# Spreading two q loads of a rotary-embedding score kernel unevenly over the sixteen DMA engines

## The chip, the cores and the metric

The kernel runs on one core of a Trainium2 chip. The core has TensorE (PE) with its weight loads (PEld), VectorE (DVE), ScalarE (ACT), GpSimd (POOL) and SyncE (SP), and sixteen DMA engines that move data between the chip's memory and the core's on-chip memory. SP, ACT and POOL issue DMAs; the sixteen engines carry them out. The metric is the time of one execution on the device in microseconds: the median of five runs.

## The reference

q and k are 16 batches x 512 positions x 16 heads x 64 floats. Both get a rotary embedding (cos and sin per position, 32 each), and then, for every batch and every position s, the 16 heads at s are multiplied with the head vectors of k. The `einsum` pairs equal heads only, so each batch and head gives a 512 x 512 matrix of scores over positions.

```python
q1, q2 = q[..., :half_dim], q[..., half_dim:]
q_rot = np.concatenate([q1 * cos_q - q2 * sin_q,
                        q1 * sin_q + q2 * cos_q], axis=-1)
...                                            # k_rot in the same way
scores = np.einsum('bshd,bthd->bsht', q_rot, k_rot)
```

The inputs are 2 x 32 MiB, the output 256 MiB, all float32: 67 MB are read and 268 MB written.

## The kernel before, in words

**Tiling.** A batch of q or k lies in on-chip memory as 128 partitions (rows) x 4 slots x 1024 floats: position 4p + c is row p, slot c. A row of a whole load is therefore 16 KB that lie together in memory, and a slot of a row is 4 KB. There are two buffers for q and two for k (`inb`, L219), used in turn by batch: batch 1 and batch 3 share a buffer, and so on.

**Steps.** There are 64 steps, one for each slot of each batch. In a step `scores` (L392) makes eight pairs of matmuls (L409), ACT copies each pair from PSUM to a stage buffer `st` (L418), and after the eighth copy SP issues one store of 4 MB (L426). There are three stage buffers; a copy into one waits until the store that used it before has landed. In the first four steps (batch 0) the store is cut into four of 1 MB (L422), and two of the stage buffers are in use. Beside this, DVE applies the embedding to slots for later steps (`rope`, L335: two products and a sum of 1.2 us each), and PE transposes them (L360), with copies from PSUM by DVE or ACT (L378).

**Loads.** Batch 0 comes in four smaller loads (`load_units`, L247). Batches 1 and up come whole, by `load` (L264), 2 MB each, on SP's queue among the stores: k and q of batch 1 at the start (L441, L442), the others when a buffer comes free (L475, L482, L508, L510). SP works in the order of the program: a DMA behind one that waits is issued later. What has been issued on SP's queue is carried out on each DMA engine in that order.

**Rows and engines.** A whole load or store of 128 rows puts 8 rows on each of the sixteen engines. A load with another number of rows is spread over fewer engines when the count doesn't divide by 16. The kernel uses this for four q loads (`RELIEVED`, L260: batches 5, 8, 11 and 14). There GpSimd issues the load of 120 rows, each as two halves of 8 KB (`halves`, L289), in its own queue (q0 in the profile), beside SP's queue (q1). A tiny load of five rows ahead of it (`move_cursor`, L282) makes GpSimd's spreading begin at engine 5, so that the fifteen engines 5 to 15 and 0 to 3 get eight rows each and engine 4 (`SLOW`, L262) none. The last 8 rows come in two ways: for batches 5 and 11 (even count) SP loads them (L302), one row each on eight engines; for 8 and 14 (odd count) GpSimd loads them ahead of the 120, after a tiny load of eight rows, on engines 8 to 15 (L296 to L298).

**Waits.** Every operation is put on a list with keys that it reads and writes, and `Plan.resolve` (L38) works out from them who waits for whom. The keys of a loaded buffer are made per slot: `in` for the rows of the main load, `in rest` for the remaining ones; a reader of a slot waits for both (`src_keys`, L304).

Of the kernel before, what the change touches and what calls it, by code (L numbers as in the profile page):

```python
# [7 lines left out]
PE, ACT, DVE, POOL, SP = "PE", "ACT", "DVE", "POOL", "SP"  # L8
# [170 lines left out]
def kernel(  # L179
# [8 lines left out]
    nc = tc.nc  # L188
# [4 lines left out]
    B, S, H, D = q.shape  # L193
    HD = D // 2
    P = 128
    C = S // P
# [9 lines left out]
    dram = {  # L206
        "q": q.rearrange("b (p c) h d -> b p c h d", c=C),
        "k": k.rearrange("b (p c) h d -> b p c h d", c=C),
    }
# [19 lines left out]
    def one(f):  # L229
        def emit():  # L230
            a = f()
            return a, a

        return emit

    def dma(engine, e, dst, src, sem, reads=(), writes=(), also=()):
        plan.add(engine, one(lambda: e.dma_start(dst, src)), reads, writes, sem=sem, also=also)  # L237
# [22 lines left out]
    RELIEVED = {("q", 5): 0, ("q", 8): 1, ("q", 11): 2, ("q", 14): 3}  # L260
# [3 lines left out]
    def load(which, b):  # L264
        if b >= B:
            return
        t = inb[which][b % 2]
        sem = f"in_{which}{b % 2}"
        rows = [("in", which, b % 2, c) for c in range(C)]
        rest = [("in rest", which, b % 2, c) for c in range(C)]  # L270
        if (which, b) not in RELIEVED:
            dma(SP, nc.sync, t.rearrange("p c (h d) -> p c h d", h=H), dram[which][b], sem, writes=rows + rest)
            return

        n, E, F = 120, C * H * D, C * H * D // 2
        x = RELIEVED[which, b]
        d = dram[which][b]  # L280

        def move_cursor(k):  # L282
            y = tiny[0]
            tiny[0] += 1
            src = bass.AP(q.tensor, 512 * y, [(512, k), (64, 2), (1, 2)])
            dst = scratch[:k, 4 * y : 4 * y + 4].rearrange("p (a b) -> p a b", a=2)
            dma(POOL, nc.gpsimd, dst, src, "cursor", writes=[("scratch", y)])

        def halves(lo, hi, keys, sem):  # L289
            src = bass.AP(d.tensor, d.offset + lo * E + F, [(E, hi - lo), (-F, 2), (1, F)])  # L290
            v = t[lo:hi]
            dst = bass.AP(v.tensor, v.offset + F, [(v.ap[0][0], hi - lo), (-F, 2), (1, F)])
            dma(POOL, nc.gpsimd, dst, src, sem, writes=keys)

        plan.add(POOL, None, (), rows)
        if x % 2:  # L296
            move_cursor(8)
            halves(n, P, rest, f"rest{x}")  # L298
        move_cursor(SLOW + 1)
        halves(0, n, rows, f"part{x}")  # L300
        if not x % 2:
            dma(SP, nc.sync, t[n:].rearrange("p c (h d) -> p c h d", h=H), d[n:], sem, writes=rest)  # L302

    def src_keys(which, n):  # L304
        if n < C:
            return [("unit", which, n)]
        return [(name, which, n // C % 2, n % C) for name in ("in", "in rest")]

    def src_also(which, n):
        return unit_keys(which, n) if n < C else ()  # L310
# [1 line left out]
    def rope(which, n):  # L312
# [9 lines left out]
        else:  # L322
# [7 lines left out]
            adds = [(x4, swapped)]  # L330
        xs, xc = x.rearrange(sv, **k2), x.rearrange(sv, **k1)
        keys, more = src_keys(which, n), src_also(which, n)

        def tt(o, a, b, op, reads, writes):
# [14 lines left out]
    def transposed(which, n, g, engine):  # L349
        m = banks[0] % 2  # L350
        banks[0] += 1
        bank = ps_t[m]
        if n < C:
            srcs = [units[which, n][:, x, P * g : P * (g + 1)] for x in range(4)]
        else:
            t = inb[which][n // C % 2]
            srcs = [t[:, n % C, P * (4 * g + x) : P * (4 * g + x + 1)] for x in range(4)]

        def emit():
            done = [nc.tensor.transpose(bank[:, x, :], srcs[x], ident) for x in range(4)]  # L360
            return done[0], done[-1]

        plan.add(PE, emit, src_keys(which, n) + ["ident"], [("bank", m)], also=src_also(which, n))
        src = bank
        if which == "q":
            dst = qTb[n % 2][:, 4 * g : 4 * g + 4, :]
            keys = [("qT", n % 2, 4 * g + x) for x in range(4)]
        else:
            b = n // C
            if n < C:  # L370
                dst = kTb[b % 2][:, 2 * n + g].rearrange("p (t c) -> p t c", c=C)
                src = bank.rearrange("p c t -> p t c")
                keys = [("kT", b % 2, 2 * n + g, c) for c in range(C)]
            else:
                dst = kTb[b % 2][:, 4 * g : 4 * g + 4, P * (n % C) : P * (n % C + 1)]
                keys = [("kT", b % 2, 4 * g + x, n % C) for x in range(4)]
        copy = nc.scalar.copy if engine == ACT else nc.vector.tensor_copy
        plan.add(engine, one(lambda: copy(out=dst, in_=src)), [("bank", m)], keys)  # L378
# [59 lines left out]
    for head, heads in ((0, G), (G, H - G)):  # L438
        load_units("k", head, heads)
        load_units("q", head, heads)  # L440
    load("k", 1)  # L441
    load("q", 1)  # L442
    plan.add(POOL, one(lambda: nc.gpsimd.memset(ident, 0.0)), (), ["ident"])
    plan.add(
# [15 lines left out]
    for i in range(C):  # L460
        plan.step = i
        if i < C - 1:
            dve = rope("k", i + 1) + rope("q", i + 1) + rope("k", C + i)
            nxt = [("k", i + 1), ("q", i + 1)]
        else:
            dve = rope("q", C) + rope("k", C + i) + rope("q", C + 1) + rope("k", 2 * C)
            nxt = [("q", C), ("k", C + i)]
        for p in range(HP):
            scores(i, p)
            if p in (0, 1) and i > 0:  # L470
                run(dve[:1])
                dve = dve[1:]
                transposed("k", C + i - 1, p, DVE)
            if p == 3 and i < 2:
                load("kq"[i], 2)  # L475
            if p in (2, 6):
                m = len(dve) - (4 if p == 2 else 2) - (2 if i == C - 1 else 0)
                run(dve[:m])
                dve = dve[m:]
                tr_act(*nxt.pop(0))  # L480
        run(dve)
# [65 lines left out]
```

## Time and profile before

| what | us |
|---|---|
| median of 5 runs | 799.25 (798.51 to 799.48) |
| profiled execution: its own time | 799.38 |
| profiled execution: span from first to last instruction | 797.6 |
| PE busy / ACT busy / DVE busy | 685.0 / 562.7 / 545.2 |
| SP's waits for ACT's copies ahead of stores | 715.8 |
| from issue to landing, median: 4 MB store / 2 MB load of q on SP | 25.6 / 29.3 |
| from issue to landing, median: 120-row load by GpSimd | 32.1 |

How to read it: a busy time is the sum over an engine's instructions. The profile's DMA row gives for 40 equal slices of the span the mean busy share of the sixteen DMA engines in tenths, 9 standing for 90% or more, and the row below it the GB/s that they moved. The queue table gives packets, megabytes and the share of sixteen engines' span that the packets took. The chain of waits goes back from the last instruction to what released it, step by step. The table by stage gives for each stretch its length, each engine's busy time and number of instructions, the granted TensorE clock, the DMA share and GB/s. All times count from the first instruction of the span. The trace also holds a record of each DMA packet: its queue, start, duration and bytes, though not the engine that carried it, and the time of each engine's report of a landed DMA.

### The profile page before, as it was taken

The page shows a single profiled execution, that of the slowest core. Times are in us where ns is not written, and L with a number is a line of the kernel's source. Part 1 is how long each engine was busy: PE and PEld are TensorE (multiplying, and loading weights), DVE is VectorE, ACT ScalarE, POOL GpSimd, SP SyncE. Part 2 cuts the span into 40 slices and gives each one's busy share as a digit, 9 for nine tenths or more (in the row PEclk, how much of TensorE's full clock was granted, in tenths as well). Part 3 has the DMA queues.
Part 4 walks back from the last instruction along what each step waited for, and adds up shares of the span by engine and source line. Part 5 has one row for each costly group of instructions (what it writes and reads, how often), then busy time and mean ns, then how long its engine had stood idle before and what let it go on. Part 6 is the DMA issues. An engine that isn't in the chain of part 4 may idle for free.

```text
span 797.6 us, 8197 instructions
## 1 busy us (share of the span) xinstructions
PE 685.0 (86%) x3072; PEld 296.2 (37%) x3072; DVE 545.2 (68%) x516; ACT 562.7 (71%) x647; POOL 8.4 (1%) x18
## 2 busy tenths in 40 slices
PE   3989999888988979899797997979879799789960
PEld 2444444333433434344343443434334344334420
DVE  6999988566776768568585775858758488575400
ACT  2978887775867768488585785868757687677860
POOL 0000000000000000100000000000000100000000
PEclk9999999997998999899898898989989899998995
DMA  9999999999999999999999999999999999999995
GB/s 343 420 423 438 428 415 422 430 428 432 427 419 429 435 431 431 431 428 410 433 427 439 426 438 428 418 433 432 432 429 432 431 427 414 427 439 411 436 425 247
DMA packets 18513, 335.87 MB, mean 421 GB/s; under 512 B 2128, under 2 KB 3408, under 8 KB 4432
## 3 DMA queue, kind: packets, MB, share of 16 engines
q1 hardware_dynamic: 16832, 327.42, 96.4%
q0 software_dynamic: 1376, 8.13, 2.4%
q10 hardware_dynamic: 288, 0.13, 0.1%
q8 instruction: 6, 0.10, 0.0%
q14 instruction: 11, 0.09, 0.0%
HBM read 67.24 MB, written 268.44 MB: 421 GB/s over the span
## 4 chain that ended last, share of the span: by engine, by line
DMA 47%; PE 37%; DVE 6%; ACT 6%; issue 1%; ACTq 0%; DVEq 0%; SPq 0%
DMA out_dram<-st 47%; PE ps L409 28%; PE bank L360 9%; ACT st L418 6%; DVE part L335 2%; DVE st L335 2%; DVE k_sb L335 1%; DVE q_sb L335 1%; DMA sin_t<-in_sin_dram 0%; DVE kT L378 0%; DVE qT L378 0%; ACTq L237 0%; ACT ss_t L455 0%; ACT ss_t L454 0%; ACTq L110 0%
## 5 line engine op out<-in xcount | busy, mean ns | idle before, releaser
L418 ACT COPY st<-ps 128x1024 f32<-128x1024 f32 x512 | 495.9, 1018 | 196.7 <-DMA out_dram<-st 101.2
L409 PE MATMUL ps<-kT,qT 64*128 64x512 f32 x2048 | 542.9, 646 | 71.7 <-ACT st L418 71.5
L409 PEld LDWEIGHTS ps<-kT,qT 64*128 64x128 f32 x2048 | 182.2, 195 | 261.4 <-issue 131.6
L378 DVE COPY qT<-bank 128x512 f32<-128x512 f32 x118 | 81.5, 691 | 197.5 <-PE bank L360 197.5
L360 PEld LDWEIGHTS bank<-ident,q_sb 128*128 128x128 f32 x480 | 55.3, 151 | 101.7 <-issue 98.2
L360 PE MATMUL bank<-ident,q_sb 128*128 128x128 f32 x480 | 86.4, 307 | 1.0 <-DVE q_sb L335 1.0
L360 PEld LDWEIGHTS bank<-ident,k_sb 128*128 128x128 f32 x480 | 50.5, 141 | 93.4 <-DVE k_sb L335 45.8
L360 PE MATMUL bank<-ident,k_sb 128*128 128x128 f32 x480 | 78.7, 287 | 1.2 <-DVE qT L378 0.8
L378 ACT COPY kT<-bank 128x512 f32<-128x512 f32 x122 | 72.4, 597 | 6.7 <-PE bank L360 6.7
L335 DVE TENSOR_TENSOR part<-q_sb,ss_t 128x1024 f32<-128x1024 f32 x60 | 73.5, 1225 | 3.2
L335 DVE TENSOR_TENSOR k_sb<-k_sb,cos_t 128x1024 f32<-128x1024 f32 x60 | 73.5, 1225 | 2.0
L335 DVE TENSOR_TENSOR q_sb<-q_sb,cos_t 128x1024 f32<-128x1024 f32 x60 | 73.5, 1225 | 2.1
L335 DVE TENSOR_TENSOR k_sb<-k_sb,part 128x1024 f32<-128x1024 f32 x60 | 73.5, 1225 | 2.1
L335 DVE TENSOR_TENSOR part<-k_sb,ss_t 128x1024 f32<-128x1024 f32 x60 | 72.9, 1216 | 0.3
L335 DVE TENSOR_TENSOR q_sb<-q_sb,part 128x1024 f32<-128x1024 f32 x60 | 72.9, 1215 | 0.0
L360 PE MATMUL bank<-ident,st 128*128 128x128 f32 x64 | 10.7, 317 | 13.3 <-DVE st L335 13.3
L360 PEld LDWEIGHTS bank<-ident,st 128*128 128x128 f32 x64 | 8.3, 161 | 18.7 <-DVE st L335 17.7
L335 DVE TENSOR_TENSOR part<-st,ss_t 128x1024 f32<-128x1024 f32 x8 | 9.8, 1223 | 6.4 <-ACT ss_t L455 6.0
L335 DVE TENSOR_TENSOR st<-st,part 128x512 f32<-128x512 f32 x16 | 11.0, 690 | 0.5
L237 POOL DMA_DIRECT2D scratch<-in_q_dram x6 | 3.6, 600 | 616.0 <-PE bank L360 616.0
L335 DVE TENSOR_TENSOR st<-st,cos_t 128x1024 f32<-128x1024 f32 x8 | 9.8, 1225 | 0.3
L378 ACT COPY qT<-bank 128x512 f32<-128x512 f32 x10 | 5.7, 616 | 3.5 <-PE bank L360 3.5
(11 smaller groups left out, 11.0 us busy)
## 6 DMA issues: line engine op xcount, KB each, us to landing
out_dram<-st SPq DMA_DIRECT2D x60, 4096.0 KB, 25.6
k_sb<-in_k_dram SPq DMA_DIRECT2D x15, 2048.0 KB, 27.2
q_sb<-in_q_dram SPq DMA_DIRECT2D x11, 2048.0 KB, 29.3
out_dram<-st SPq DMA_DIRECT2D x16, 1024.0 KB, 12.4
q_sb<-in_q_dram POOLq DMA_DIRECT2D x4, 1920.0 KB, 32.1
st<-in_k_dram SPq DMA_DIRECT2D x1, 1536.0 KB, 9.1
st<-in_q_dram SPq DMA_DIRECT2D x1, 1536.0 KB, 12.3
st<-in_k_dram SPq DMA_DIRECT2D x1, 512.0 KB, 4.9
```

The source lines that it names most:

```text
L237: plan.add(engine, one(lambda: e.dma_start(dst, src)), reads, writes, sem=sem, also=also)
L335: plan.add(DVE, one(lambda: nc.vector.tensor_tensor(o, a, b, op=op)), reads, writes, also=more)
L360: done = [nc.tensor.transpose(bank[:, x, :], srcs[x], ident) for x in range(4)]
L378: plan.add(engine, one(lambda: copy(out=dst, in_=src)), [("bank", m)], keys)
L409: nc.tensor.matmul(out=ps[:, r, :], lhsT=lhs[lo:hi, :], rhs=rhs[lo:hi, :], start=True, stop=True)
L418: plan.add(ACT, one(lambda: nc.scalar.copy(out=so, in_=si)), [("ps", y)], [("st", s, p)])
```

## The change

Two loads are spread otherwise.

The first whole q load (batch 1, at the start) was one DMA of 128 rows x 16 KB. It becomes three on SP's queue: slots 0 to 2 of all 128 rows (12 KB a row); slot 3 of 116 rows (4 KB a row), which go to engines 0 to 3; slot 3 of the last 12 rows. Each has its own semaphore.

The last GpSimd load (batch 14) had 8 rows on engines 8 to 15 by one GpSimd DMA and 120 rows by another. Now GpSimd loads 99 rows, nine each on engines 5 to 15, after the tiny load of five rows; the tiny load of eight rows and the second GpSimd load go. SP loads the other 29 rows in two DMAs, of 13 and of 16 rows, behind the store that is issued ahead of them. A third key, `in more`, stands for the 16 rows, and readers of a slot wait for it too.

```diff
+        if (which, b) == ("q", 1):
+            def view(lo, hi, c0, c1):
+                return (
+                    t[lo:hi, c0:c1].rearrange("p c (h d) -> p c h d", h=H), dram[which][b][lo:hi, c0:c1]
+                )
+            dma(SP, nc.sync, *view(0, P, 0, C - 1), sem, writes=rows[:-1] + rest[:-1])
+            dma(SP, nc.sync, *view(0, 116, C - 1, C), f"{sem}_116", writes=rows[-1:])
+            dma(SP, nc.sync, *view(116, P, C - 1, C), f"{sem}_12", writes=rest[-1:])
+            return
...
-        n, E, F = 120, C * H * D, C * H * D // 2
         x = RELIEVED[which, b]
+        last = x == len(RELIEVED) - 1
+        n, E, F = 99 if last else 120, C * H * D, C * H * D // 2
...
-        if x % 2:
+        if x % 2 and not last:
             move_cursor(8)
             halves(n, P, rest, f"rest{x}")
         move_cursor(SLOW + 1)
         halves(0, n, rows, f"part{x}")
-        if not x % 2:
-            dma(SP, nc.sync, t[n:].rearrange("p c (h d) -> p c h d", h=H), d[n:], sem, writes=rest)
+        if last or not x % 2:
+            ends = (n, n + 13, P) if last else (n, P)
+            for y, (lo, hi) in enumerate(zip(ends, ends[1:])):
+                dma(
+                    SP, nc.sync, t[lo:hi].rearrange("p c (h d) -> p c h d", h=H), d[lo:hi],
+                    sem if y == 0 else f"{sem}_rest{y}",
+                    writes=rest if y == 0 else [("in more", which, b % 2, c) for c in range(C)],
+                )
...
-        return [(name, which, n // C % 2, n % C) for name in ("in", "in rest")]
+        return [(name, which, n // C % 2, n % C) for name in ("in", "in rest", "in more")]
```

## The prediction

> **What bounds the kernel now.** I read the page from the top. The span, the DMA rows of the slices and the queue table come first: the sixteen DMA engines are the busy resource.
>
> ```profile
> span 797.6 us, 8197 instructions
> PE 685.0 (86%) x3072; PEld 296.2 (37%) x3072; DVE 545.2 (68%) x516; ACT 562.7 (71%) x647; POOL 8.4 (1%) x18
> ...
> DMA  9999999999999999999999999999999999999995
> ...
> q1 hardware_dynamic: 16832, 327.42, 96.4%
> q0 software_dynamic: 1376, 8.13, 2.4%
> ```
>
> The DMA row is at 9 from the first slice to the last but one, and PE is the next resource at 86%. The chain of waits, in order of time, says the same from 116 us on: one store of 25 to 29 us per round. These are its last rounds:
>
> ```profile
> 655.00 26.66 DMA out_dram<-st
> ...
> 692.25 24.17 DMA out_dram<-st
> ...
> 747.54 18.63 DMA out_dram<-st
> ```
>
> The table by stage shows one place where the mean falls, at the end, when only stores are left:
>
> ```profile
> 116.00:400.00 284.00, 252.18 (x1116) 107.42 (x1114) 197.71 (x186) 202.99 (x233) 3.93 (x6) 0.93 1.00 428
> 700.00:727.00 27.00, 24.01 (x102) 10.27 (x102) 19.32 (x19) 18.45 (x22) 0.00 (x0) 0.87 1.01 434
> 727.00:740.00 13.00, 12.75 (x62) 5.34 (x58) 5.44 (x6) 11.21 (x14) 0.00 (x0) 1.00 0.94 403
> ```
>
> A mean over sixteen engines hides which engine is last, so I went to the trace's packet records (queue, start, duration, bytes). On one engine a packet starts 3 or 4 ns before the one ahead of it ends, so the records thread into sixteen chains, and each chain carries exactly 8 packets of every whole store and load. Five chains hold the tiny cursor rows of every GpSimd load (engines 0 to 4), and one of these five carries no 8 KB halves: engine 4, the one the code skips. Three more have the cursor rows of the odd loads only (5 to 7). When the chains end, before the last:
>
> ```
> engine 4                 0.0 us (last packet ends at 794.9)
> next: one of 8-15        2.8      one of 5-7   3.0
> two of 8-15 4.5, 5.3     one of 5-7 4.6        two of 0-3  5.0, 5.5
> all others               5.1 to 7.0
> ```
>
> One inference is in this: at 652.0 us two chains end 7 ns apart, and I went on with the one that keeps the long store packets. Engine 4 is steadily slow: a 32 KB store packet takes 1213 ns elsewhere and mostly 1216 to 1260 on it, about 0.25 us lost per 12 us, 18 us in all by 652 us. It is never idle from 14 us on but for 0.4 us. At 727 us seven other engines idle for 1.0 to 2.4 us, because the next store waits for a buffer that engine 4 holds, while engine 4 has 6.5 us of backlog. So the time is the sum of engine 4's own packets, and any other engine matters only if it becomes later than it.
>
> **The change, engine by engine.** By the row counts, 116 = 4 x 29 rows go to engines 0 to 3, 12 rows to 0 to 11, 13 rows to 0 to 12, 16 rows one each, and 99 = 11 x 9 rows to 5 to 15. The trace of before has the like: each 8-row SP load put one 16 KB packet on each of eight engines, and the 120 and 8 row GpSimd loads used 15 and 8.
>
> *First q load (L272), engine 4.* Before: 8 packets of 16 KB at 611 ns = 4.89 us. After: 8 of 12 KB at about 460 (between the 309 of 8 KB and the 611 of 16 KB), one of 4 KB at about 159 (between 121 for 3 KB and 309), and a semaphore packet of 9 ns = 3.85. So -1.04 us.
>
> *Last GpSimd load (q 14), engine 4.* Before: no rows. After: one row of the 13 and one of the 16: 2 x (611 + 9) = +1.24 us. Both earlier SP remainders (at 211 and 506 us) also stretched the store packet ahead of the row, on engine 4 alone, to 1813 and 1815 ns: 0.6 us each. For two rows back to back the bounds are 0 (the engines whose row cost only 611) and 1.2; I take one stall, +0.6, since only the first row follows a store.
>
> *The second GpSimd load and its cursor row go.* On engine 4 store packets are stretched near the end of each GpSimd load: 1672, 1676, 1487, 1456 ns in this one, 1.3 us above its usual 1240; 1.7 in the other two-part load and 0.9 to 1.2 in the one-part ones. Taking the last load as one-part: -0.4, between 0 and -1.3 (all of it gone).
>
> Sum for engine 4: -1.04 + 1.24 + 0.6 - 0.4 = **+0.4 us**, between -1.1 and +1.4.
>
> *Does another engine take over?* Engines 5 to 7: q1 -1.04, q14 +2 halves (0.62) +1.24 = +0.8, so the later of them still ends 2.6 us before engine 4. Engines 8 to 11: -1.04, no extra halves, +1.24: +0.2. 12: 0. 13 to 15: -1.2 + 0.6 = -0.6. Engines 0 to 3: q1 8 x 460 + 30 x 159 against 4.89, +3.6; q14 16 halves go (-4.94), two rows come (+1.24): -0.1. None is last, and no gain can pass the 2.2 to 2.8 us at which the next engine decides.
>
> *What hides the rest.* Engines 0 to 3 run some 3.5 us later from 24 us to the last GpSimd load, so stores land later where these are then the slowest: by 2 us up to 80 us, by about 1 us around 230 to 290 us, not at all later, since engine 4 and its neighbours were 5 to 9 us behind anyway. That delays the copies into the freed stage buffer and the next store; engine 4's own backlog covers it. Without that cover it would cost those 1 to 2 us. The first q load lands at 25.0 us, then at about 28.5, and DVE first reads it at 52.2. q 14 landed at 658.8; two more halves on each engine, each alternating with a store packet (2 x 1.5 us), less the 1.1 us by which GpSimd issues it earlier, give about 661; DVE first reads it at 663.2, and if it were late, the qT copies behind it on DVE, then PE, wait; DVE idles 7.7 us at 678, which bounds the harm. The four extra SP issues (0.3 to 0.6 us each) fall where SP then waits for ACT, up to 20.9 and 644.5 us. After the first q load the queue is thin: the first store is issued at 20.9, the second at 24.2; engine 4 comes 1.04 us sooner (23.3 instead of 24.4), needs the second at 25.8, and the issue takes about 0.9 us to reach the engines: free, at worst 0.3 us.
>
> *Two rules against the trace.* The packet rows make engine 4 the late one. The Trainium skill (DMA: Bandwidth & Descriptors, Latency and other measured facts) says that engines 7 and 15 are usually the slower ones. If 15 were last, the change would give -0.6 us, about 798.6; the trace has the slow chain among engines 0 to 4, so I go by it. Second, the first q load lands at 25.0 us and nothing reads it before 52.2. The same page's Rules for kernel authors ask that a transfer use all 16 engines, and warn of outer sizes that confine it to few; this speaks against 116 rows on four engines, and where something waited for that load it would cost the 3.5 us, 802.8. No row shows anything that does.
>
> **The rivals.**
> - *Slower.* Reads beside a GpSimd load are dearer on engine 4. For: load packets of 1434 to 1511 ns instead of 611 stand there, and the loads next after GpSimd's cost engine 4 0.8 to 1.9 us. Against: its rows at 211 and 506 us took 611. If both rows cost 1.5 us and both stall: -1.04 + 2 x (1.5 + 0.6) = +3.2, about 802.4. It passes +1.6 once the two rows cost over 2.65 us together, nothing else saved.
> - *Faster.* With four engines out of GpSimd's last load and one load fewer, the stretch goes (-1.3), no row stalls, and the stall of the k load after it (1.4 to 1.9 us on engine 4) shrinks to the 0.8 of the mildest: -1.04 + 1.24 - 1.3 - 0.9 = -2.0, about 797.2. For: engines 5 to 7 paid no stall for their rows. Against: all four GpSimd loads show the stretch.
> - *The rows do not go where the title says.* If the 116 rows spread over all engines, engine 4 does not get its 1.04 us early: +1.4, 800.7. Against: the 8-row loads on eight engines.
>
> **How the numbers follow.** The profiled execution took 799.38 us (span 797.6 and 1.8 around it), 0.13 above the median of 799.25, to which I add: 799.25 + 0.4 = 799.65, say 799.7. A measurement of this kernel can tell about 0.2%, 1.6 us, from no change: 797.65 to 800.85. Chances: forecast 0.52 (its own range 798.1 to 800.7), rows not as said 0.03, slower rival 0.25, faster rival 0.20. The first two lie within 0.2%, so same 0.55. For 8 in 10 the range goes half way into both rivals: 797.5 to 801.6.
>
> **What would show it.** In the landings of the last store, one engine still ends 2 us or more behind the next. In the packets, a chain with long store packets carries two 16 KB rows between 640 and 660 us, a store packet of about 1.8 us before the first. Issues: q loads of 1536, 464 and 48 KB early; 208, 256 and a GpSimd 1584 KB late. Stores up to 80 us land with a spread of 4 instead of 2.5 us. I am wrong if the last chain is another engine, if engine 4 has gaps, or if DVE waits for a q load.

## The result, and the profile after

| | kernel before | changed kernel |
|---|---|---|
| median (executions) | 798.73 (80) | 799.82 (44) |
| lowest to highest | 797.46 to 800.89 | 796.54 to 806.91 |
| executions above 801 us | 0 of 80 | 17 of 44 |
| profiled execution, its span | 799.38, 797.6 | 798.52, 796.7 |

The ratio is 1.0025, with a 95% interval from 1.0016 to 1.0034: slower by 2 us in the mean (800.82 against 798.85), just past the 0.2% that a measurement of this kernel can tell. The median is 0.1 us from the forecast, but the times are not what it described: the change did not add 0.4 us to every execution. More than half of them (23 of 44) still take 800 us or less, three of them less than any of before, and 17 take 3 to 8 us longer than the mean of before. The profiled execution is one of the short ones, so the page of after alone can't show what costs. It does show most of the steps. Top of the page:

```profile
span 796.7 us, 8201 instructions
PE 681.3 (86%) x3072; PEld 293.0 (37%) x3072; DVE 545.1 (68%) x516; ACT 562.3 (71%) x647; POOL 7.3 (1%) x16
...
DMA  8999999999999999999999999999999999999996
...
q1 hardware_dynamic: 17034, 327.90, 96.8%
q0 software_dynamic: 1328, 7.65, 2.3%
```

GpSimd's queue q0 carries 0.48 MB less and SP's queue as much more. The DMA row differs from that of before in its first and last slice only. The last three long waits of the chain, all still for stores:

```profile
654.37 27.82 DMA out_dram<-st
...
694.39 21.71 DMA out_dram<-st
...
744.41 20.87 DMA out_dram<-st
```

The table by stage (stretch, its length, busy time of PE, PEld, DVE, ACT and POOL with instructions, clock, DMA share, GB/s):

```profile
116.00:400.00 284.00, 248.66 (x1106) 105.35 (x1104) 197.95 (x186) 201.07 (x231) 3.93 (x6) 0.93 1.00 429
700.00:727.00 27.00, 26.47 (x130) 11.74 (x130) 22.48 (x21) 22.67 (x28) 0.00 (x0) 1.00 1.01 435
727.00:740.00 13.00, 12.75 (x64) 5.40 (x62) 6.64 (x8) 11.37 (x13) 0.00 (x0) 1.00 1.01 436
```

The dip at 727 us is gone (share 1.01 and 436 GB/s, where before it was 0.94 and 403), and the end came only 0.9 us sooner: before, the engines that idled there were not the ones that decided. The DMA issues by size show that the rows go where the diff says:

```profile
q_sb<-in_q_dram POOLq DMA_DIRECT2D x1, 1584.0 KB, 31.6
...
q_sb<-in_q_dram SPq DMA_DIRECT2D x1, 1536.0 KB
...
q_sb<-in_q_dram SPq DMA_DIRECT2D x1, 464.0 KB
...
q_sb<-in_q_dram SPq DMA_DIRECT2D x1, 256.0 KB, 27.8
q_sb<-in_q_dram SPq DMA_DIRECT2D x1, 208.0 KB
...
q_sb<-in_q_dram SPq DMA_DIRECT2D x1, 48.0 KB
```

Threaded into sixteen chains like those of before, the packet records of this execution end as follows: engine 4 at 794.0 us (0.9 sooner), three of engines 0 to 3 at 793.7, 791.5 and 791.4. (The four are known by their 48 halves, where the others have 66 or 68; the fourth can't be told from neighbours at 663 and 667 us, so its end, 787 to 790, is not certain.) Before, engines 0 to 3 ended 5 to 7 us ahead of engine 4, at 788.0 to 789.9; one of them is now 0.3 us ahead of it. There lies the difference between the short and the long executions, as the runs below show.

### The profile page after: what moved, and what is told of

Its sections match the earlier page's. It is cut to its first block, busy times and chain, and to the rows that moved or that the text cites. A ratio compares the mean times of both kernels' runs of the same rounds, so it can differ in the third digit from the quotient of the medians.

```text
span 796.7 us, 8201 instructions
## 1 busy us (share of the span) xinstructions
PE 681.3 (86%) x3072; PEld 293.0 (37%) x3072; DVE 545.1 (68%) x516; ACT 562.3 (71%) x647; POOL 7.3 (1%) x16
## 4 chain that ended last, share of the span: by engine, by line
DMA 47%; PE 37%; DVE 6%; ACT 6%; issue 1%; ACTq 0%; DVEq 0%; SPq 0%
DMA out_dram<-st 47%; PE ps L428 28%; PE bank L379 9%; ACT st L437 6%; DVE part L354 2%; DVE st L354 2%; DVE k_sb L354 1%; DVE q_sb L354 1%; DMA sin_t<-in_sin_dram 1%; DVE kT L397 0%; DVE qT L397 0%; ACTq L237 0%; ACT ss_t L474 0%; ACT ss_t L473 0%; ACTq L110 0%
## 5 line engine op out<-in xcount | busy, mean ns | idle before, releaser
L379 PE MATMUL bank<-ident,q_sb 128*128 128x128 f32 x480 | 84.2, 301 | 1.0 <-DVE q_sb L354 1.0
```

## The experiments

The kernels of this part were timed against the kernel before on the same chip.

**The change once more, and each half of it alone.** `again` is the changed kernel. `first_only` has only the split of the first q load:

```diff
-        last = x == len(RELIEVED) - 1
-        n, E, F = 99 if last else 120, C * H * D, C * H * D // 2
+        n, E, F = 120, C * H * D, C * H * D // 2
```

with the branch for the first load kept and all of the last load as before. `last_only` takes that branch out and keeps the last load's new form:

```diff
-        if (which, b) == ("q", 1):
-            ...
-            return
```

> The changed kernel once more, for a second profile and for the spread of its times. Theory 'stretch' (an engine that gets no rows of a GpSimd load has its store packets stretched while that load runs, by some 2.5 us, so engines 0 to 3 get back only about half of the 4.9 us that the last load was to give them): in an execution over 801 us one of engines 0 to 3 ends last, in one under 799 engine 4 does; the stretched store packets of engines 0 to 3 stand between 638 and 652 us. Theory 'two rows' (the two SP rows on engine 4 decide): engine 4 ends last in every execution. Median 799.8, single times 796.5 to 807.

> Only the first q load is split; the last GpSimd load is as before. Stretch: engines 0 to 3 start 3.6 us late but get their relief in no load either way, and end where they ended before plus 3.6 us, 2 to 3 us ahead of engine 4, or level with it at worst; engine 4 has up to 1.0 us less to do. Time 0.3 to 1.0 us under the kernel before, 797.7 to 798.4, spread as narrow as before. Rival 'late four' (the early delay alone makes engines 0 to 3 last): 800 or more, with the wide spread. Two rows: 1.0 us under the kernel before, as all that costs is gone.

> Only the last GpSimd load is changed (99 rows on engines 5 to 15, 29 rows by SP); the first q load is whole. Stretch: engines 0 to 3 lose 16 halves (4.9 us) and gain two rows with a stalled store (about 2.4) and the stretch (2.5), so they end about where they did, 5 us ahead; engine 4 gets two rows and one stalled store, +2.3, less up to 1 us of stretch: 1.3 to 2 us over the kernel before, 800 to 800.8, narrow spread. Late four: as before, 798.7. Two rows: the same +1.3 to +2.3.

| kernel | median | range | above 801 | ratio to before |
|---|---|---|---|---|
| again | 800.71 | 797.47 to 807.46 | 5 of 12 | 1.0028 (1.0008 to 1.0047) |
| first_only | 802.98 | 798.48 to 808.32 | 7 of 11 | 1.0048 (1.0025 to 1.0071) |
| last_only | 798.83 | 797.57 to 799.7 | 0 of 11 | 0.9999 (0.999 to 1.0008) |

The theory of the stretched stores fell with `first_only`, which it expected below 798.4 us with a narrow range; what came is its rival, the late four engines. The two rows that SP puts on engine 4 cost nothing that shows in `last_only`. The first half alone costs 4 us and brings the spread. The second half alone changes nothing; beside the first it seems to give some 2 us of the 4 back, but the intervals of `again` and `first_only` overlap, and that gain is not shown. The profiled executions of `again` and `first_only` are long ones (spans 802.3 and 803.3 us), and there the late engines can be seen. Landings of the 4 MB stores, numbered by step: the last of the sixteen reports (us), and in brackets how far the earliest engine was ahead of it:

```
store    before         after          again          first_only
o4       91.0 (3.0)     94.0 (5.2)     93.6 (6.2)     94.3 (7.1)
o11     175.8 (3.9)    177.1 (4.8)    176.8 (5.5)    177.8 (6.8)
o23     323.8 (6.3)    324.1 (6.1)    326.4 (9.3)    326.9 (10.1)
o27     371.8 (5.0)    373.3 (5.9)    376.8 (10.4)   376.8 (10.3)
o47     618.8 (9.1)    618.5 (7.9)    625.3 (11.3)   624.6 (11.5)
o63     795.3 (7.1)    794.5 (7.4)    800.0 (7.7)    801.0 (8.9)
```

In `after` the last landing starts 3 us later than before and is level by o23. In `again` it is level with `after` at o11, 2.3 us behind at o23, 3.5 at o27 and 6.8 at o47. Who is last can be read from the records: engine 4 is the chain with the 1216 to 1260 ns store packets. In `again` it carries them (57 of its 81 stores after 690 us) and ends 3.4 us ahead of the last chain; two chains without such packets end 3.4 and 3.1 us after it, a third 0.8, and these are chains without halves in the last GpSimd load, so of engines 0 to 3. In `first_only` the three last chains end 4 us and more behind all others, and have no such packets. So engines 0 to 3 set the end of the long executions.

Where they lose the time: in each chain I took the duration of 16 KB load packets above 611 ns and of store packets above 1213 ns, for packets that end between 230 us and the landing of o23, where no GpSimd load runs:

```
             the latest chains (us of loads + stores)        the others
after        0.22 + 0   0.01 + 0   0.26 + 0                   0 to 0.33 in all
again        1.76 + 0.20   1.67 + 0.26                        0 to 0.56 (engine 4: 1.9, its slow stores)
first_only   1.43 + 0.17   1.52 + 0.26   1.56 + 0.17          0 to 0.55 (engine 4: 2.1, its slow stores)
```

The packets are single loads of 700 to 1300 ns and a store of 1290 to 1380 ns ahead of them. In these two executions the engines that are late lose more, and so become later still. By the end of the same store on each chain, engines 0 to 3 were 4.0 to 4.9 us behind the mean of engines 5 to 15 at o11 in `again`, and 7.0 to 11.8 us at o38; in after it was 3.1 to 3.9 and 3.7 to 5.8 us. That lateness brings the losses is not shown by these executions alone. Further on nearly all engines take part: between 535 and 625 us each chain of `again` lost 0.7 to 3.2 us, the chains of after other than engine 4 at most 0.35. The table by stage for 535 to 625 us, first of the profiled execution of after (431 GB/s, as before had):

```profile
535.00:625.00 90.00, 82.16 (x361) 34.94 (x362) 63.35 (x60) 67.52 (x78) 1.35 (x2) 0.92 1.00 431
```

The same stretch in `again`:

```profile
535.00:625.00 90.00, 78.82 (x350) 33.27 (x346) 62.47 (x59) 61.42 (x71) 0.00 (x0) 0.92 1.00 424
```

And in `first_only`:

```profile
535.00:625.00 90.00, 77.71 (x348) 32.94 (x344) 62.39 (x59) 61.68 (x72) 0.00 (x0) 0.94 1.01 424
```

The DMA share, second last number, is the same and hides the loss: the engines are busy, but move 424 instead of 431 GB/s, which is 1.6% of 90 us, 1.5 us.

Why does it happen in some executions only? At o11 `again` differs from after by 0.7 us of spread (5.5 against 4.8) and by little else. In the profiled execution of after the cosine and sine tables came late, by the head of the chain of waits (start, duration, what):

```profile
1.32 5.00 DMA sin_t<-in_sin_dram
```

against 3.95 before. The same piece of the chain in `again`:

```profile
1.32 3.84 DMA sin_t<-in_sin_dram
```

The first store was then issued at 21.95 us instead of 20.74, and engines 4 to 15 ran dry while engines 0 to 3 still had their rows, as the table by stage of after has it (DMA share and GB/s last; before, 442 and 410 GB/s):

```profile
22.00:23.00 1.00, 1.00 (x9) 0.81 (x9) 0.97 (x2) 1.00 (x2) 0.00 (x0) 1.00 0.90 311
23.00:24.00 1.00, 1.00 (x6) 0.39 (x4) 0.90 (x2) 0.97 (x3) 0.00 (x0) 1.00 0.89 295
```

That late store took about 1 us off the lead of the others: at o7 engines 0 to 3 were 4.1 to 5.0 us behind their mean in `again`, 3.2 to 4.1 in after. It is no effect of the change: a kernel without the split first load (`four_rows`, below) waited 4.90 us for the same table. That this decides between a short and a long execution is a lead from one pair of executions, and is not shown.

**Is it the four engines, or the small pieces?** `first_even` has the same three DMAs and the same 4 KB rows, evenly spread:

```diff
-            dma(SP, nc.sync, *view(0, 116, C - 1, C), f"{sem}_116", writes=rows[-1:])
-            dma(SP, nc.sync, *view(116, P, C - 1, C), f"{sem}_12", writes=rest[-1:])
+            dma(SP, nc.sync, *view(0, 112, C - 1, C), f"{sem}_112", writes=rows[-1:])
+            dma(SP, nc.sync, *view(112, P, C - 1, C), f"{sem}_16", writes=rest[-1:])
```

> As first_only (the first q load in three DMAs, 4 KB rows in the fourth slot), but the fourth slot goes by 112 + 16 rows instead of 116 + 12, which is seven and one row on every one of the sixteen engines. Theory 'late four' (the cost of first_only, 803.0 us, comes from engines 0 to 3 being 5.3 us behind): nobody is behind, so 798.4 to 799.2 us, with a narrow range like before's. Rival 'small pieces' (three DMAs of short rows, issued while the queue is thin, cost by themselves): 801 us or more, with a wide range.

799.41 us (798.61 to 802.17; 2 of 12 above 801, where the kernel before had 1 of 35 on this chip, at 802.89), ratio 1.0011 (0.9998 to 1.0024): 0.2 us above the range of the first theory, and well short of the rival's 801. Most of the cost goes with the concentration; up to 0.2% may belong to the pieces, which this run can't tell from nothing.

**Does it matter when the four are delayed?** `late_first` splits the q load of batch 13 instead of batch 1:

```diff
-        if (which, b) == ("q", 1):
+        if (which, b) == ("q", 13):
```

> As first_only, but the load that is split (slots 0 to 2, then 116 rows of slot 3 on engines 0 to 3, then 12) is the q load of batch 13, issued around 585 us, where engines 0 to 3 are 3.5 to 7 us ahead of engine 4 in the profile of before, instead of that of batch 1. The packets are the same in number and size. Theory 'lag feeds on itself' (an engine that runs over 8 us behind the earliest loses another 1 to 1.6 us per batch in stalled loads and stretched stores, so an early delay grows): the delay finds slack and has no time to grow: 797.5 to 799 us, narrow. Rival 'fixed sum' (the four engines have that much more to carry, wherever it stands): as first_only, 802 to 803.5 us.

798.68 us (797.47 to 799.73; 0 of 11 above 801), ratio 0.9996 (0.9984 to 1.0008). The same packets on the same engines cost 4 us at the start and nothing at 590 us: a fixed sum is out. It does not by itself tell growth from slack, since at 618 us engines 0 to 3 have their whole lead to lose, and the landings were up to 2.4 us later than before at o50 (658.1 against 655.7) before engine 4 was the last again.

**Does early relief stop the growth?** `relief_early` is the change with the new form of the GpSimd load at batch 5 instead of batch 14:

```diff
-        last = x == len(RELIEVED) - 1
+        last = x == 0
```

> The change with its second part moved from the last GpSimd load (batch 14, 640 us) to the first (batch 5, 190 us): there GpSimd loads 99 rows on engines 5 to 15 and SP 13 + 16 rows; batch 14 is loaded as before the change. The sums of packets per engine are those of the change, to within one load of 8 rows. Theory 'lag feeds on itself': engines 0 to 3 catch up 4 to 5 us at 200 us and lose nothing more: 798.2 to 799.3 us, narrow. Rival 'fixed sum': as the change, 799.8 to 800.7 us, with its wide range.

798.84 us (797.72 to 800.04; 0 of 11 above 801), ratio 1.0 (0.9989 to 1.0012). Its profiled execution starts with a spread of 5.9 us at o11, more than `again` (5.5), and stands at 5.1 us at o13, 5.2 at o23 and 5.0 at o27, where `again` has 7.7, 9.3 and 10.4. Engines 0 to 3, 4.3 to 5.1 us behind the mean of the others at o11, are 2.5 to 4.8 us behind at o38. With nearly the same sums per engine as in the change, the delay neither grows nor costs.

**And is there a dose that costs nothing?** `first_76` puts 76 rows (19 each) on engines 0 to 3 instead of 116:

```diff
-            dma(SP, nc.sync, *view(0, 116, C - 1, C), f"{sem}_116", writes=rows[-1:])
-            dma(SP, nc.sync, *view(116, P, C - 1, C), f"{sem}_12", writes=rest[-1:])
+            dma(SP, nc.sync, *view(0, 76, C - 1, C), f"{sem}_76", writes=rows[-1:])
+            dma(SP, nc.sync, *view(76, P, C - 1, C), f"{sem}_52", writes=rest[-1:])
```

> As first_only, with a smaller dose: slot 3 of the first q load goes by 76 rows (19 of 4 KB on each of engines 0 to 3) and 52 rows (four each on engines 0 to 12) instead of 116 and 12. At the measured 0.18 us a row engines 0 to 3 start 3.5 us behind the others instead of 5.3. Theory 'lag feeds on itself' (what costs is being 8 us and more behind the earliest engine, which this delay does not reach): 798.3 to 799.5 us, and hardly an execution above 801 us (first_only: 7 of 11). Rival 'in proportion' (19/29 of the 4.2 us that first_only costs): 801 to 802 us, half of the executions above 801.

797.99 us (797.01 to 799.37; 0 of 11 above 801; 0.3 us below the range of the first theory), ratio 0.9996 (0.9987 to 1.0005). Two thirds of the dose cost nothing, so the cost isn't in proportion. The bound that I set for it, 8 us behind the earliest engine, is not the right one: the profiled execution reached 10.3 us at o47, and that of before 9.1. What these runs support is the delay of engines 0 to 3 before the first GpSimd load: of the kernels with the four GpSimd loads of before, those in which it stays as small as in `first_76` (a spread of 4.6 us at o11) or is taken back there do not become long. A spread at o11 alone doesn't decide: `late_first`, where engines 0 to 3 have no extra rows by then, had 5.9 there in its profiled execution.

**Is engine 4's sum the time otherwise?** `four_rows` is the kernel before with SP's 8-row remainders cut in two, so that they go to engines 0 to 3 and none to engine 4:

```diff
-            dma(SP, nc.sync, t[n:].rearrange("p c (h d) -> p c h d", h=H), d[n:], sem, writes=rest)
+            for y, lo in enumerate((n, n + 4)):
+                dma(
+                    SP, nc.sync, t[lo : lo + 4].rearrange("p c (h d) -> p c h d", h=H), d[lo : lo + 4],
+                    sem if y == 0 else f"{sem}_rest{y}",
+                    writes=rest if y == 0 else [("in more", which, b % 2, c) for c in range(C)],
+                )
```

> The kernel before, with the 8-row remainder that SP loads for batches 5 and 11 cut into two DMAs of 4 rows, so that they go to engines 0 to 3 (two rows each) and none to engines 4 to 7. If engine 4's own sum is the time of the kernel before, it loses two rows of 0.62 us and the two stalls of 0.6 to 1.1 us ahead of them: 2.4 to 3.4 us less, cut at 2.8 us where the next engine ends: 795.9 to 796.6 us. Rival (what engine 4 saves is lost elsewhere, or it only idles): within 0.8 us of before, 798 to 799.5 us.

798.59 us (797.1 to 799.88), ratio 0.9992 (0.998 to 1.0005). The 2.4 us did not come. Engine 4 is still the last and still never idle, but its terms moved. From 50 us to the end, in the profiled executions:

```
             16 KB load packets   above 611 ns   stores above 1213 ns   engine 4 ends
before             178               7.47 us          22.45 us             794.9
four_rows          176               8.72             23.61                795.4
last_only          180               6.20             22.50                794.1
after              180               4.96             22.43                794.0
```

Beside two rows less (1.2 us) stand 1.25 us more of stalled loads and 1.16 us more of stretched stores; in `last_only`, beside two rows more, 1.27 us less of stalls. That the one brings the other is not shown: these are single executions, that of `four_rows` is the longest of its eleven (799.88 us), and two executions of the changed kernel differ by as much: 4.96 us of stalled loads on engine 4 in after, 8.49 in `again`. The interval also leaves room for a gain of up to 1.6 us.

**GpSimd rows in one piece.** `whole_rows` is the kernel before with GpSimd's rows as 16 KB instead of two halves of 8 KB:

```diff
-            src = bass.AP(d.tensor, d.offset + lo * E + F, [(E, hi - lo), (-F, 2), (1, F)])
+            src = bass.AP(d.tensor, d.offset + lo * E, [(E, hi - lo), (1, E)])
...
-            dst = bass.AP(v.tensor, v.offset + F, [(v.ap[0][0], hi - lo), (-F, 2), (1, F)])
+            dst = bass.AP(v.tensor, v.offset, [(v.ap[0][0], hi - lo), (1, E)])
```

> The kernel before, but GpSimd loads whole rows of 16 KB instead of two halves of 8 KB, in all four loads. If engine 4's stretch comes from the tiny packets that GpSimd's queue puts on an engine without rows, one for each half elsewhere, half as many make about half the stretch: engine 4 loses about 1.2 us instead of 2.3 to 2.6 per load, and ends up to 2.8 us earlier (the next engine bounds it): 796 to 797.5. If it comes from the reads of the other engines, the bytes are the same and so is the stretch: 798.7, within 0.8.

811.53 us (810.87 to 813.26), ratio 1.0164 (1.015 to 1.0178): both expectations missed. The last landing is 1.4 us later than before at o15, 6.7 at o25, 8.3 at o38 and 14.5 at o50, behind one load after the other. The edit does more than cut the rows otherwise: it also moves the spreading. In the packet records the chain with the 1216 to 1260 ns store packets, which has none of GpSimd's rows before, now carries 8, 9, 8 and 9 of them in the four loads, between its stores, and ends last, 4.9 us after the next. The engine without rows is now another one, which has none of SP's rows either and so is one of 8 to 15. The 34 rows at 0.61 us are 21 us of work from which the slow engine was spared before, so the 12.7 us can't be put down to the size of the pieces: a row took 0.61 us in the median of the first three loads, and 0.92 in that of the last. On the stretch the run does tell something. The engine without rows had about half as many tiny packets, 10 or 11 in the first and in the third load instead of 18, and its store packets were still stretched by 2.5 and 2.7 us. That speaks against the number of tiny packets as the cause of the stretch, though it was read on another engine than 4.

**Versions that might beat both.** `five_loads` and `six_loads` change only the list of relieved batches:

```diff
-    RELIEVED = {("q", 5): 0, ("q", 8): 1, ("q", 11): 2, ("q", 14): 3}
+    RELIEVED = {("q", 3): 0, ("q", 6): 1, ("q", 9): 2, ("q", 12): 3, ("q", 14): 4}
```

and `{("q", 3): 0, ("q", 5): 1, ("q", 7): 2, ("q", 9): 3, ("q", 11): 4, ("q", 13): 5}`. `combined` is `five_loads` with the split of `first_76` and the remainders of `four_rows`.

> The kernel before with five GpSimd loads instead of four (batches 3, 6, 9, 12, 14 instead of 5, 8, 11, 14). If the sum of engine 4's own packets is the time: one load more takes 8 rows (4.9 us) from it and costs it 2.3 to 2.6 us of stretched stores and 0.8 to 1.9 us of stalls in the load behind: 0.5 to 1.7 us less, 797.1 to 798.2 us. Rival (what is taken from engine 4 comes back as stalls, as with the four rows): 798.5 us or more.

> The kernel before with six GpSimd loads (batches 3, 5, 7, 9, 11, 13) instead of four. five_loads measured 0.8 us less than before for one load more. Theory 'sum of engine 4': another step of the same size, 796.5 to 797.5 us, until the next engine (2.8 us ahead of it in the profile of before) decides. Rival (six loads cost the other fifteen engines as much in stalls as they take from engine 4): no better than five, 797.6 us or more.

> five_loads with the two small reliefs that cost nothing alone: the first q load's slot 3 by 76 + 52 rows, and the 8-row remainders of SP (batches 3, 9, 14) as two DMAs of 4 rows on engines 0 to 3. Theory 'sum of engine 4': 0.5 us from the first and three times 1.2 us (a row and its stall) from the second, less what comes back; cut where the next engine ends: 795.5 to 797.2 us. Rival (savings of a row or two on engine 4 come back as stalls in the loads behind): as five_loads, 797.4 to 798.2 us.

| kernel | median | range | above 801 | ratio to before |
|---|---|---|---|---|
| five_loads | 797.61 | 796.35 to 799.08 | 0 of 11 | 0.9988 (0.9979 to 0.9997) |
| six_loads | 798.23 | 797.75 to 802.01 | 1 of 11 | 1.0 (0.9989 to 1.001) |
| combined | 803.37 | 800.09 to 810.78 | 10 of 11 | 1.0063 (1.0043 to 1.0084) |

`five_loads` is the fastest kernel of this study, 0.12% below the kernel before. Six are no better: there, as in `five_loads`, engine 4 is no longer the last chain. `combined` adds two edits that cost nothing alone, misses both of its expectations, and takes as long as `first_only`: both edits put their rows on engines 0 to 3 (3.5 us at the start, two rows at each of three loads). Even in its fastest execution, the profiled one, the four last chains are those with the six more rows of SP, and the other twelve engines, 4 among them, end 4.6 us and more ahead of the last.

## Why the prediction was right or wrong

**The number.** 799.7 against a measured 799.82, and a ratio at the edge of "no difference". The closeness is luck: the forecast added 0.4 us to 799.25, the median of five runs, while the median of the 80 is 798.73, so the change measured 1.1 us in the median and 2.0 in the mean. And it is a right number from a mechanism that was half right: the forecast's own story, engine 4 a little later in every execution, is not what happens.

**Engine 4, +0.4 (-1.1 to +1.4).** In the profiled execution it ends 0.9 us sooner. By terms: the first q load's packets were as costed (465 ns for 12 KB, 161 for 4 KB), but the 1.04 us did not arrive, because the store behind was issued late; in `again`, where it was not, engine 4 ends o4 1.1 us sooner than before. The two rows cost 0.61 to 0.81 us each, as costed. The store ahead of them was stretched to 2335 ns, by 1.1 us instead of 0.6: near the 1.2 that the prediction gave as the bound for two stalls, though, as it said, "only the first row follows a store". In this execution the same packet was stretched to 2.1 to 2.3 us on engines 0 to 3 too, and to 1.34 us at most on the engines that had GpSimd rows. The rest of the stretch near the last GpSimd load shrank by more than the 0.4 that I took: four store packets of 1456 to 1676 ns before, three of 1331 to 1438 ns after, some 1 us less. So these two terms came to about 0 where I had +0.2. What made engine 4 earlier is the load behind (batch 15 of k): 1.5 us less stall, a term that I had put into the faster rival alone.

**"Does another engine take over?" failed.** This is the step: "Engines 0 to 3: q1 8 x 460 + 30 x 159 against 4.89, +3.6; q14 16 halves go (-4.94), two rows come (+1.24): -0.1. None is last". In the profiled execution three of them end 1.5 to 3.8 us later than the latest of them did before; in `again` two of them end 3 us and more behind engine 4, in `first_only` three end 4 us and more behind it. Three terms were wrong. A row of 4 KB took 182 to 192 ns in the mean, not 159, so that engines 0 to 3 fall 5.3 us behind their neighbours instead of 4.6. The relief is smaller than the rows taken away: in the last load, without GpSimd's rows, their store packets were stretched by 2.3 to 3.1 us in after (about 1 us of it ahead of SP's rows), against at most 0.14 in the three loads before, so from o48 to o52 they gained 1.2 to 2.5 us on the mean of engines 5 to 15 in after and 4.5 to 4.8 in `again`, not the 5.5 that the terms give against engines 5 to 7. Above all the sum took the delay as a constant from 24 to 640 us, while in the long executions it grew.

**"What hides the rest" failed with it.** I had the stores up to 80 us land with a spread of 4 us (measured 4.3 to 5.9 in after; 5.0 to 6.6 in `again`) and called the delay covered by engine 4's backlog, 1 to 2 us without that cover. The cover was there at first: the last landing was 3 us late at o4 and level at o23. What I left out is that a late engine can pay more for its loads, as it did in both long executions that were profiled.

**The thin queue** was taken as "free, at worst 0.3 us". The queue did run dry in the profiled execution, for about 1 us, but through a late table that the change does not cause, and by the comparison with `again` it may rather have helped there.

**The rest held.** The rows went where the title says. The reader of q 14 never waited: the waits of DVE in after between 640 and 700 us (total, times, longest) are all for PE:

```profile
DVE qT L397 <- PE bank L379: 18.1, 10, 7.7
```

The first three q issues took SP 4.77 us, over at 9.2, long before its next work at 21.95. No rival told of engines 0 to 3 as the last: the slower one put its 3 us on engine 4's rows, which cost 0.6 to 0.8 us each. The two rules weighed: the late engines were 4 and then 0 to 3, nothing here speaks of 7 or 15. What the Trainium skill says (DMA: Bandwidth & Descriptors, Rules for kernel authors) on using all sixteen engines was nearer to these runs than my row against it: no reader waited for that load, and alone it still cost 4 us through the engines' later work, though nothing measurable where it came late, was smaller or was relieved soon.

**What stays open.** Why a late engine's load packets take 700 to 1300 ns, alone or with others, is not shown; that the two go together rests on two long profiled executions and on `relief_early`. Where between 76 and 116 rows the cost begins was not measured, nor why two rows less on engine 4 bring no gain that shows. What 16 KB pieces alone would cost was not measured either, since `whole_rows` moved the spared engine too.

## What to carry to other kernels

Where all engines are busy, a load that is put on a few of them may not be paid when it lands but for as long as these are behind, and the debt can grow; here it was cheap late in the kernel or with a relief soon after. A sum of one engine's packets tells who ends last, but a row taken from it is worth what the run shows, not its duration: here two rows of 0.6 us less on the last engine gave no gain that shows. After an edit to a load's shape, look in the packets whether each engine still gets the rows that it had: in `whole_rows` it did not. And look at all the executions' times before the profile: here the profiled one was a short one, and what cost stood in the others.

## What the runs showed of the hardware that was not expected

- An engine without rows in a GpSimd load gets as many 4-byte packets on that queue as the others get halves, and some of its store packets take 1350 to 1727 ns: 1.8 to 2.5 us per load on engine 4 in the four loads of before, 1.2 to 2.2 us on engines 0 to 3 in the one load of after where they have none, the store ahead of SP's rows not counted. With about half as many tiny packets (`whole_rows`) it was 2.5 and 2.7 us in two loads.
- A single 16 KB row by SP takes 0.6 us itself. On an engine without rows in the GpSimd load it also stretches the store packet ahead of it: one row to 1.81 us (engine 4 in before), two rows to 2.1 to 2.3 us (engines 0 to 4 in after). On engines with GpSimd rows that packet mostly kept its 1213 ns in these two executions.
- A DMA share of 1.00 does not mean full speed: 431 and 424 GB/s had the same share.
